# Block products for twelve slices of layer 0's second feed-forward, and where the weight sums are made

## The chip, the cores and the metric

The kernel runs on one core of a Trainium2 chip. The metric is the device time of one execution in microseconds, the median of several runs. TensorE does the matmuls and accumulates in PSUM banks of 512 float32 for each partition; VectorE (DVE) and ScalarE (ACT) do the elementwise work, each strictly in its own program order; GpSimd (POOL) here copies marks and starts some DMA transfers; SyncE (SP) starts the other transfers.

## What is computed

One inference step of a two-layer decoder over 1,024 prompt tokens and 8 sample rows. Layer 0 has a gated linear recurrence beside attention into 256 memory tokens, layer 1 stick-breaking attention beside memory attention; each is followed by the SwiGLU feed-forward that the change is about, in which `D_MODEL` is 1024 and `D_FF` is 2816:

```python
def swiglu(h, w_gu, w_down):
    gate, up = jnp.split(h @ w_gu, 2, axis=-1)
    return (jax.nn.silu(gate) * up) @ w_down
...
        h = h + rmsnorm(mix, g[1])
        h = h + rmsnorm(swiglu(rmsnorm(h, g[2]), w_gu[l], w_down[l]), g[3])
```

Everything is float32.

## The kernel before

**Tiling.** Activations lie transposed, features on the 128 partitions and tokens along the free axis. The tokens are two groups: group 0 holds 512 prompt tokens, group 1 the other 512 and the 8 sample rows, 520 columns that are worked on as two halves of 260 (`PW[1]`). A float32 product is made of reduced-precision ones (`float32r`): weight and activation are each split into a high and a low part, and three matmuls stand for one (high by high, high by low, low by high).

**A plain slice.** The feed-forward takes its 2,816 hidden features in 22 slices of 128. For one slice `split_w` (L250) loads weights as raw tiles of 128 x 512 from the pool `wraw` (5 tiles, on SP's queue), makes the high part on ScalarE (L260) and the low part on VectorE (L261) into the pool `wspl` (5 tiles); `proj` (L266) multiplies (L274). Gate and up have two such tiles each, so a slice of group 1 has four weight tiles, each used for 4 x 3 x 2 = 24 matmuls of 260 columns: 96 in all. The result lies in a `mm` tile, two PSUM banks wide, of which the pool `mmp` has two. `silu` (L284) works by exponential and logarithm.

**Parts.** The 22 slices are cut into parts of 5, 5, 4, 4 and 4 (`PARTS`). After a part's slices come its eight down projections, which add into the residual rows `R` (`class ffn`, L688; the addition is L447 in `evac_raw`). The part is the unit in which feed-forwards are interleaved with attention: each stage is a generator, and `weave` takes turns between generators by the number of steps given with each, so the program order of every engine is fixed when the program is written. The order of the whole is at L1488 to L1525. `f1 = ffn(1, 0, o1.x)` (L1500), layer 0's feed-forward for group 1, is the one whose last three parts the change touches; its first two run beside `b0.sb()` and `b0.mem()`, layer 1's attention for group 0 (matmuls L862 and L903, maximum L867, exponential L873, scaling L877 and L879, transposition L889).

**Block products.** Layer 1's feed-forward for group 1 (`class ffn_w`, L617) makes all slices but the first four in another way. The gate and up projections of a slice are one product of a 2 x 2 block matrix of weights (gate and up by first and second 512 features of `D_MODEL`) with a 2 x 2 block matrix of activations (first and second 512 features by first and second 260 columns). `gate_up_w` (L524) makes it of 7 block products in place of 8. Four of the seven weights are sums of blocks, three are blocks themselves; four of the seven operands are sums of activation blocks, three the blocks themselves. A block product has one weight tile of 128 x 512, used for 4 x 3 = 12 matmuls of 260 columns, so a slice has 84. Its seven products go into four accumulators, `pa` to `pd`, and between the products ScalarE writes negated copies into an accumulator before it is accumulated further (L559 and L562), and silu of `pa` (L565), a copy of `pd` (L568), an addition (L570), a subtraction (L572) and a second silu (L574) follow:

```python
        product(pa, 0, True)
        nc.scalar.activation(pb[:, :h], pa[:, :h], AF.Copy, scale=-1.0)
        product(pd, 1, True)
        product(pb, 2)
        nc.scalar.activation(pc[:, :h], pb[:, :h], AF.Copy, scale=-1.0)
        product(pa, 3)
        ...
        product(pb, 4)
        ...
        nc.vector.tensor_add(gt[:, h:n], dt[:, h:n], pb[:, :h])
        product(pc, 5)
        nc.vector.tensor_sub(gt[:, :h], pc[:, :h], dt[:, h:n])
        product(pb, 6)
```

The silu there is ScalarE's own table function, whose table is loaded by an instruction of its own (`ACT_TABLE_LOAD`) when the function changes. In that stage the other PSUM pools are closed, and each accumulator has two banks of its own (`quads`, L1523). Raw tiles come from `wraw` and, every second one, from halves of the pool `apool`; split tiles come from `wspl` and, three of eight, from `cpool`. Operand sums are made by `sums_w` (L326): for each of four blocks of 128 features 4 additions, 4 subtractions and 4 splits.

**Weight sums.** `weight_sums` (L588) makes the sums of weight blocks in DRAM (`wsum`), a part at a time, by eight transfers on GpSimd's queue: copies (L608) and transfers that add to what is there (L606). Each waits for a mark: ScalarE copies a column (L602) of what was made last, the number `self.now` that `ffn` keeps, into a small tile `rr`, GpSimd copies that (L603), and the transfer is issued after it. Before, the 40 transfers for layer 1's 22 slices are interleaved with parts 0 to 4 of `f1`.

**PSUM around the change.** Eight banks: `mmp` two tiles of two banks, `smp` three small banks (`S()`: attention's scores and transpositions), `nsp` one.

Of the kernel before, what the change touches and what calls it, by code (L numbers as in the profile page):

```python
# [24 lines left out]
def tile_decoder(  # L25
# [61 lines left out]
    def Q(i):  # L87
        return single[0].tile([P, 512], F32, tag=f"q{i}", name=nm("q"))
# [139 lines left out]
    def chain(*gens):  # L228
        for g_ in gens:
            yield from g_  # L230
# [16 lines left out]
    def sv(ap, g):  # L247
        return ap[:, :G] if g == 0 else ap.rearrange("p (a n) -> p a n", a=2)

    def split_w(W, k0, nk, m0):  # L250
        out = []
        for a in range(0, nk, 4):
            n = min(4, nk - a)
            raw = wraw.tile([P, 4, P], F32, tag="w", name=nm("w"))
            nc.sync.dma_start(
                raw[:, :n, :],
                W[(k0 + a) * P : (k0 + a + n) * P, m0 : m0 + P].rearrange("(k p) m -> p k m", p=P),
            )
            ws = wspl.tile([P, 2, 4, P], F32R, tag="ws", name=nm("ws"))
            nc.scalar.copy(ws[:, 0, :n, :], raw[:, :n, :])  # L260
            nc.vector.tensor_sub(ws[:, 1, :n, :], raw[:, :n, :], ws[:, 0, :n, :].bitcast(F32))  # L261
            for i in range(n):
                out.append((ws[:, 0, i, :], ws[:, 1, i, :]))
        return out
# [58 lines left out]
            out.append(x)  # L323
            yield

    def sums_w(xs, ops):  # L326

        n, h = NG[1], PW[1]  # L330
        for k in range(4):
            x0, x1 = xs[k], xs[k + 4]
            y = YT()
            if k % 2 == 0:
                z, u = YT(), YT()
            o = (k % 2) * h

            def full(x, c):
                t = B()
                nc.vector.tensor_add(t[:, :h], x[:, 0, c : c + h].bitcast(F32), x[:, 1, c : c + h].bitcast(F32))  # L340
# [13 lines left out]
            yield  # L354

    def YT():
        return xpool.tile([P, 2, NG[1]], F32R, tag="x0", name=nm("y"))

    def wo_tiles(g):
# [161 lines left out]
        split_to((mt[:, 0, :n], mt[:, 1, :n]), sg[:, :n])  # L521
        return mt, last

    def gate_up_w(l, f, ops, spl, raws):  # L524

        h, n = PW[1], NG[1]
        part, o = part_of(f)
# [26 lines left out]
                        start=(first and k == 0 and wi == 0), stop=(k == 3 and wi == 2), skip_group_check=True,  # L554
                    )

        pa, pb, pc, pd = (Q(i) for i in range(4))
        product(pa, 0, True)
        nc.scalar.activation(pb[:, :h], pa[:, :h], AF.Copy, scale=-1.0)  # L559
        product(pd, 1, True)  # L560
# [10 lines left out]
        product(pc, 5)  # L571
        nc.vector.tensor_sub(gt[:, :h], pc[:, :h], dt[:, h:n])  # L572
        product(pb, 6)
        nc.scalar.activation(sg[:, h:n], gt[:, :h], AF.Silu)  # L574
# [4 lines left out]
        return mt  # L579

    sums = {}

# [2 lines left out]
            if f0 <= f < f0 + nf:  # L585
                return i, (f - f0) * P

    def weight_sums(l, parts, after):  # L588

        for i in parts:  # L590
            f0, nf = PARTS[i]
            w = nf * P
            s1, s2, s3, s4 = (tc.dram_tile([512, w], F32, name=nm("wsum")) for _ in range(4))
            sums.setdefault(l, {})[i] = (s1, s2, s3, s4)
            a11, a12 = (w_gu[l][r : r + 512, f0 * P : f0 * P + w] for r in (0, 512))
            a21, a22 = (w_gu[l][r : r + 512, DFF + f0 * P : DFF + f0 * P + w] for r in (0, 512))
            for d, a, add in (
                (s3, a11, False), (s1, a21, False), (s3, a21, True), (s1, a22, True),
                (s2, s3, False), (s2, a22, True), (s4, s2, False), (s4, a12, True),
            ):  # L600
                tok = small([P, 1], tag="rr")
                nc.scalar.copy(tok, after())  # L602
# [12 lines left out]
    class ffn_w:  # L615


        def __init__(self, l, x, plain):
            self.g, self.l, self.x, self.ops, self.plain, self.n, self.r, self.pi = 1, l, x, [], plain, 0, 0, 0
            self.R = self.acc = None  # L620
            self.half = []
            self.sums = sums_w(x, self.ops)

        def spl(self):
            self.n += 1
# [13 lines left out]
        def part(self, pi):  # L639
# [4 lines left out]
            for j in range(nf):  # L644
# [5 lines left out]
                        for _ in range((1, 2, 1, 0)[j]):  # L650
                            next(self.sums, None)
                else:
                    mids.append(gate_up_w(l, f0 + j, self.ops, self.spl, self.raws))
                yield
            if pi == 0:
                self.R = R_one()
# [29 lines left out]
            yield from finish_rows(self)  # L686

    class ffn:  # L688
        def __init__(self, g, l, xt, rows=False):
            self.g, self.l, self.xt, self.rows = g, l, xt, rows  # L690
            self.R = self.acc = None

        def part(self, pi):
            g, l = self.g, self.l
# [2 lines left out]
            last = pi == len(PARTS) - 1  # L697
            mids = []
            for j in range(nf):
                pg = proj(g, w_gu[l], 0, ND, (f0 + j) * P, self.xt)  # L700
                sg = silu(None, pg, g)
                pu = proj(g, w_gu[l], 0, ND, DFF + (f0 + j) * P, self.xt)
# [4 lines left out]
                self.now = sg[:, 0:1]  # L707
                yield
            if pi == 0:
                self.R = R_one()  # L710
            if last:
                self.acc = small([P, WID], tag="st", bufs=3)
            for m in range(ND):
                ps = proj(g, w_down[l], f0, nf, m * P, mids)
                evac_raw(g, self.R, ps, m, self.acc, pi == 0, last)
                self.now = self.R[m][:, 0:1]
                if last and self.rows:
                    nc.scalar.activation(
                        self.R[m][:, :n], self.R[m][:, :n], AF.Copy, scale=gcol(l, 3, m)
# [1 line left out]
                    if m == 3:  # L721
                        first_half(self)
                if m % 2:
                    yield

        def finish(self, store):
# [749 lines left out]
    )  # L1476
    a0.open()
    a1 = mixer_a(1, x1)
    weave((chain(a0.gate(), a0.merge()), 8), (start(1, x1), 14))
    weave((a0.mem(), 8), (a1.fq(), 8))  # L1480
    o0 = out_proj(0, 0, M)
    drain(o0.mm(a0.xo))
    weave((o0.finish(), 17), (chain(a1.v(), a1.qm(A)), 8))
    f0 = ffn(0, 0, o0.x)
    weave((a1.core(), 22), (f0.part(0), 9))
    a1.open()
    weave((a1.sample(), 6), (a1.gate(), 4), (f0.part(1), 9))
    weave((chain(a1.merge(), a1.mem()), 12), (a1.mem_sample(), 20), (chain(f0.part(2), f0.part(3)), 16))  # L1488
    drain(f0.part(4))
    xk0, xb0 = [], []  # L1490
    o1 = out_proj(1, 0, M)
    drain(o1.mm(a1.xo, 0, 1))
# [66 lines left out]
```

## Times and profile before

| | |
|---|---|
| median of 3 runs | 2498.32 us (2496.75 to 2498.65) |
| the profiled execution | 2499.1 us, with a span of 2497.4 us |
| TensorE: busy, granted clock | 2462.8 us, 0.997 of full speed |
| VectorE, ScalarE, GpSimd busy | 1571.8, 1183.0, 98.3 us |
| moved by DMA | 358.21 MB |

Times come from one execution that the hardware profiler recorded; L274 is line 274 of the kernel before. A row of a group gives line, engine, operation, the tile written and the tiles read, their shapes, the number of instructions, then their busy time, the mean of one in ns, and the engine's idle time ahead of them with what ended it. Matmuls overlap, and their ends are modelled, so their mean is longer than the time that each adds. A row of the order of time gives start, duration, engine, line, operation and how many instructions are put together in it. A row by windows gives the window, its length, and the busy time of PE, weight loads, DVE, ACT and POOL with the number of instructions, the granted clock, the share of the DMA engines and GB/s.

### The profile page before, as it was taken

The page shows a single profiled execution, that of the slowest core. Times are in us where ns is not written, and L with a number is a line of the kernel's source. Part 1 is how long each engine was busy: PE and PEld are TensorE (multiplying, and loading weights), DVE is VectorE, ACT ScalarE, POOL GpSimd, SP SyncE. Part 2 cuts the span into 40 slices and gives each one's busy share as a digit, 9 for nine tenths or more (in the row PEclk, how much of TensorE's full clock was granted, in tenths as well). Part 3 has the DMA queues.
Part 4 walks back from the last instruction along what each step waited for, and adds up shares of the span by engine and source line. Part 5 has one row for each costly group of instructions (what it writes and reads, how often), then busy time and mean ns, then how long its engine had stood idle before and what let it go on. Part 6 is the DMA issues. An engine that isn't in the chain of part 4 may idle for free.

```text
span 2497.4 us, 40764 instructions
## 1 busy us (share of the span) xinstructions
PE 2462.8 (99%) x15565; PEld 2169.9 (87%) x15565; DVE 1571.8 (63%) x2756; ACT 1183.0 (47%) x2277; POOL 98.3 (4%) x139
## 2 busy tenths in 40 slices
PE   8999999999999999999999999999999999999998
PEld 6888988877877897999999989877787797999997
DVE  5766556655765585655544575777577648755655
ACT  5446543243433454555433454555444445564444
POOL 1000000000000000010111100022000000000000
PEclk9999999999999999999999999999999999999999
DMA  5352252233643447586678976544454234365542
GB/s 186 114 165 68 72 156 81 60 110 116 184 124 98 129 138 227 156 195 177 173 191 215 234 193 196 160 142 138 121 149 130 85 115 122 121 192 145 151 137 69
DMA packets 496110, 358.21 MB, mean 143 GB/s; under 512 B 19110, under 2 KB 443635, under 8 KB 495915
## 3 DMA queue, kind: packets, MB, share of 16 engines
q1 hardware_dynamic: 477354, 301.08, 40.5%
q0 software_dynamic: 18560, 54.53, 9.1%
q8 instruction: 122, 2.00, 0.3%
q14 instruction: 74, 0.60, 0.1%
HBM read 325.73 MB, written 75.94 MB: 161 GB/s over the span
## 4 chain that ended last, share of the span: by engine, by line
PE 88%; DVE 5%; DMA 3%; ACT 2%; issue 2%; POOL 0%; SPq 0%; DVEq 0%; ACTq 0%; POOLq 0%
PE mm L274 59%; PE q L552 7%; PE q L667 5%; PE s L1180 2%; PE q L510 2%; PE mm L1048 2%; PE s L903 1%; PE s L862 1%; PE mm L812 1%; DMA b<-qd 1%; PE mm L839 1%; DVE ws L261 1%; PE ns L957 1%; PE s L1336 1%; DMA c<-in_cache_sb_v,pidx 1%
## 5 line engine op out<-in xcount | busy, mean ns | idle before, releaser
L274 PE MATMUL mm<-x,ws 128*128 128x260 f32 (+1 forms) x7776 | 1332.9, 330 | 0.0
L274 PEld LDWEIGHTS mm<-x,ws 128*128 128x128 f32 x7776 | 1148.3, 188 | 151.5 <-issue 12.0
L260 ACT CAST ws<-w 128x512 fp32r<-128x512 f32 x712 | 420.2, 591 | 763.2 <-PE mm L274 620.2
L261 DVE TENSOR_TENSOR ws<-w,ws 128x512 fp32r<-128x512 f32 x712 | 462.5, 653 | 286.8 <-ACT ws L260 278.3
L274 PE MATMUL mm<-m,ws 128*128 128x512 f32 (+1 forms) x2112 | 393.5, 343 | 0.1
L274 PEld LDWEIGHTS mm<-m,ws 128*128 128x128 f32 x2112 | 324.4, 189 | 49.9 <-issue 2.6
L667 PE MATMUL q<-m,ws 128*128 128x260 f32 x1056 | 128.8, 283 | 0.0
L667 PEld LDWEIGHTS q<-m,ws 128*128 128x128 f32 x1056 | 127.2, 188 | 0.4 <-ACT hT L485 0.2
L543 DVE TENSOR_TENSOR ws<-w,ws 128x512 fp32r<-128x512 f32 x126 | 86.6, 691 | 61.5 <-ACT ws L542 59.3
L552 PE MATMUL q<-y,ws 128*128 128x260 f32 x864 | 112.9, 283 | 0.0
L542 ACT CAST ws<-w 128x512 fp32r<-128x512 f32 x126 | 78.0, 621 | 69.6 <-PE q L667 27.4
L552 PEld LDWEIGHTS q<-y,ws 128*128 128x128 f32 x864 | 107.6, 189 | 0.0
L291 DVE TENSOR_SCALAR t<-mm 128x512 f32<-128x512 f32 (+1 forms) x82 | 56.7, 692 | 79.6 <-PE mm L274 79.6
L447 DVE TENSOR_TENSOR r<-r,mm 128x512 f32<-128x512 f32 (+1 forms) x96 | 66.0, 688 | 61.1 <-PE mm L274 60.3
L703 DVE TENSOR_TENSOR t<-t,mm 128x512 f32<-128x512 f32 (+1 forms) x66 | 45.5, 690 | 74.2 <-PE mm L274 73.9
L295 DVE TENSOR_TENSOR t<-t,t 128x512 f32<-128x512 f32 (+1 forms) x66 | 45.8, 694 | 70.6 <-ACT t L294 70.6
L552 PE MATMUL q<-x,ws 128*128 128x260 f32 x648 | 86.3, 282 | 0.0
L552 PEld LDWEIGHTS q<-x,ws 128*128 128x128 f32 x648 | 81.3, 188 | 0.0
L314 DVE TENSOR_TENSOR st<-st,n 128x512 f32<-128x512 f32 (+1 forms) x98 | 67.1, 691 | 8.8 <-ACT n L313 7.0
L281 ACT CAST m<-t 128x512 fp32r<-128x512 f32 (+1 forms) x88 | 54.9, 624 | 18.1 <-DVE t L703 8.9
L282 DVE TENSOR_TENSOR m<-t,m 128x512 fp32r<-128x512 f32 (+1 forms) x88 | 61.0, 693 | 2.6 <-ACT m L281 1.4
L984 POOL DMA_INDIRECT c<-in_cache_sb_k,pidx x16 | 16.4, 1026 | 1170.5 <-ACT n L313 958.6
(339 smaller groups left out, 2557.9 us busy)
## 6 DMA issues: line engine op xcount, KB each, us to landing
w<-in_w_gu SPq DMA_DIRECT2D x334, 256.0 KB, 3.4
w<-in_w_down SPq DMA_DIRECT2D x160, 256.0 KB, 3.5
w<-in_w_in_a SPq DMA_DIRECT2D x80, 256.0 KB, 3.0
wsum<-in_w_gu POOLq DMA_DIRECT2D x18, 1024.0 KB, 9.5
w<-wsum SPq DMA_DIRECT2D x72, 256.0 KB, 3.8
w<-in_w_o SPq DMA_DIRECT2D x64, 256.0 KB, 2.8
wsum<-in_w_gu POOLq DMA_DIRECT2D x12, 1280.0 KB, 10.7
w<-in_w_mem_kv SPq DMA_DIRECT2D x32, 256.0 KB, 3.2
```

What stands on the lines that cost most here:

```text
L260: nc.scalar.copy(ws[:, 0, :n, :], raw[:, :n, :])
L261: nc.vector.tensor_sub(ws[:, 1, :n, :], raw[:, :n, :], ws[:, 0, :n, :].bitcast(F32))
L274: nc.tensor.matmul(ps[:, a, : PW[g]], wt, xt[k][:, xi, o : o + PW[g]], start=(k == 0 and wi == 0), stop=(k == nk - 1 and wi == 2),)
L281: nc.scalar.copy(dst[0], src)
L282: nc.vector.tensor_sub(dst[1], src, dst[0].bitcast(F32))
L291: nc.vector.tensor_scalar(sv(x, g), pv(ps, g), -44.0, None, op0=ALU.max)
L314: nc.vector.tensor_add(acc[:, :n], acc[:, :n], t[:, :n])
L447: nc.vector.tensor_add(dst, dst, pv(ps, g))
L542: nc.scalar.copy(w[:, 0, :], src)
L543: nc.vector.tensor_sub(w[:, 1, :], src, w[:, 0, :].bitcast(F32))
L552: nc.tensor.matmul(ps[:, :h], w[:, wj, k * P : (k + 1) * P], x[:, xi, :], start=(first and k == 0 and wi == 0), stop=(k == 3 and wi == 2), ...
L667: nc.tensor.matmul(pp[a][:, :h], wt, mids[k][:, xi, a * h : (a + 1) * h], start=(k == 0 and wi == 0), stop=(k == nf - 1 and wi == 2),)
```

## The change

Three things change together.

1. `f1`, layer 0's feed-forward for group 1, gets `prod=10`: its parts 2 to 4 (slices 10 to 21, twelve slices) are made by `gate_up_w`. Raw tiles come from `wraw` alone; split tiles from `wspl` and `cpool` (three of eight). Two accumulators (`pa`, `pd`) are small banks of `smp`, the two others (`pb`, `pc`) the halves of one `mm` tile. The operand sums are made in the down projections of part 1, one block after every second projection, into tiles of `apool`. ScalarE's table for exponential and logarithm is loaded again behind the last slice's gate.
2. Layer 0's weight sums for parts 2 to 4, 24 transfers, are added; they are interleaved with the memory attention, output projection and recurrence of the first half and with `f0.part(0)`. Layer 1's 40 move forward: 24 beside `f0.part(2)` to `f0.part(4)` of group 0 and 16 beside parts 0 and 1 of `f1`. In parts 2 to 4 of `f1` none are left.
3. The mark ahead of each of these transfers now reads the first column of the weight tile that was split last (`now[0]`, set in `split_w`).

```diff
+            now[0] = ws[:, 0, 0, 0:1].bitcast(F32)
...
-    def sums_w(xs, ops):
+    def sums_w(xs, ops, YT):
...
-        pa, pb, pc, pd = (Q(i) for i in range(4))
+        pa, pb, pc, pd = quads()
...
-                nc.scalar.copy(tok, after())
+                nc.scalar.copy(tok, now[0])
...
-        def __init__(self, g, l, xt, rows=False):
-            self.g, self.l, self.xt, self.rows = g, l, xt, rows
+        def __init__(self, g, l, xt, rows=False, prod=NF):
+            self.g, self.l, self.xt, self.rows, self.prod = g, l, xt, rows, prod
             self.R = self.acc = None
+            self.ops, self.n = [], 0
+            self.sums = sums_w(xt, self.ops, lambda: A(F32R))
+
+        def spl(self):
+            self.n += 1
+            if self.n % 8 in (1, 4, 6):
+                return cpool.tile([P, 2, 512], F32R, tag="c", name=nm("ws"))
+            return wspl.tile([P, 2, 512], F32R, tag="ws", name=nm("ws"))
+
+        def quads(self):
+            t = mmp.tile([P, 2, 512], F32, tag="mm", name=nm("mm"))
+            return S(), t[:, 0, :], t[:, 1, :], S()
...
+                if f0 + j >= self.prod:
+                    mt, gate = gate_up_w(
+                        l, f0 + j, self.ops, self.spl,
+                        lambda: wraw.tile([P, 4, P], F32, tag="w", name=nm("w")), self.quads,
+                    )
+                    mids.append(mt)
+                    yield
+                    continue
...
+            if last and self.prod < NF:
+                with tc.issue_after(gate.ins):
+                    nc.scalar.preload_act_table_set("natural_log_exp_and_others")
...
                 if m % 2:
+                    if f0 + nf == self.prod < NF:
+                        next(self.sums, None)
                     yield
...
+    ws = weight_sums(0, (2, 3, 4))
     weave((chain(a0.gate(), a0.merge()), 8), (start(1, x1), 14))
-    weave((a0.mem(), 8), (a1.fq(), 8))
+    weave((a0.mem(), 8), (a1.fq(), 8), (islice(ws, 6), 6))
     o0 = out_proj(0, 0, M)
-    drain(o0.mm(a0.xo))
-    weave((o0.finish(), 17), (chain(a1.v(), a1.qm(A)), 8))
+    weave((o0.mm(a0.xo), 8), (islice(ws, 6), 6))
+    weave((o0.finish(), 17), (chain(a1.v(), a1.qm(A)), 8), (islice(ws, 6), 6))
     f0 = ffn(0, 0, o0.x)
-    weave((a1.core(), 22), (f0.part(0), 9))
+    weave((a1.core(), 22), (f0.part(0), 9), (ws, 6))
...
-    weave((chain(a1.merge(), a1.mem()), 12), (a1.mem_sample(), 20), (chain(f0.part(2), f0.part(3)), 16))
-    drain(f0.part(4))
+    ws = weight_sums(1, range(5))
+    weave(
+        (chain(a1.merge(), a1.mem()), 12), (a1.mem_sample(), 20), (chain(f0.part(2), f0.part(3)), 16), (islice(ws, 16), 17)
+    )
+    weave((f0.part(4), 8), (islice(ws, 8), 8))
...
-    f1 = ffn(1, 0, o1.x)
-    ws = weight_sums(1, range(5), lambda: f1.now)
-    weave((chain(b0.sb(), b0.mem()), 24), (chain(f1.part(0), f1.part(1)), 18), (islice(ws, 16), 17))
-    weave((chain(f1.part(2), f1.part(3), f1.part(4)), 24), (ws, 24))
+    f1 = ffn(1, 0, o1.x, prod=10)
+    weave((chain(b0.sb(), b0.mem()), 24), (chain(f1.part(0), f1.part(1)), 18), (ws, 17))
+    drain(f1.part(2), f1.part(3), f1.part(4))
```

More of the change, by code (lines that the diff above doesn't have):

```diff
@@ L248, in sv @@
         return ap[:, :G] if g == 0 else ap.rearrange("p (a n) -> p a n", a=2)
+    now = [None]
     def split_w(W, k0, nk, m0):
@@ L354, in sums_w, with Y0 @@
             yield
-    def YT():
+    def Y0():
         return xpool.tile([P, 2, NG[1]], F32R, tag="x0", name=nm("y"))
@@ L522, in gate_up_q, with gate_up_w @@
         return mt, last
-    def gate_up_w(l, f, ops, spl, raws):
+    def gate_up_w(l, f, ops, spl, raws, quads):
         h, n = PW[1], NG[1]
@@ L573, in gate_up_w @@
         product(pb, 6)
-        nc.scalar.activation(sg[:, h:n], gt[:, :h], AF.Silu)
+        last = nc.scalar.activation(sg[:, h:n], gt[:, :h], AF.Silu)
         nc.vector.tensor_mul(sg[:, :h], sg[:, :h], pb[:, :h])
@@ L578, in gate_up_w @@
         split_to((mt[:, 0, :n], mt[:, 1, :n]), sg[:, :n])
-        return mt
+        return mt, last
     sums = {}
@@ L586, in part_of, with weight_sums @@
                 return i, (f - f0) * P
-    def weight_sums(l, parts, after):
+    def weight_sums(l, parts):
         for i in parts:
@@ L621, in __init__ @@
             self.half = []
-            self.sums = sums_w(x, self.ops)
+            self.sums = sums_w(x, self.ops, Y0)
         def spl(self):
@@ L652, in part @@
                 else:
-                    mids.append(gate_up_w(l, f0 + j, self.ops, self.spl, self.raws))
+                    mids.append(gate_up_w(
+                        l, f0 + j, self.ops, self.spl, self.raws, lambda: [Q(i) for i in range(4)]
+                    )[0])
                 yield
@@ L706, in part @@
                 mids.append(mt)
-                self.now = sg[:, 0:1]
                 yield
+            if last and self.prod < NF:
+                with tc.issue_after(gate.ins):
+                    nc.scalar.preload_act_table_set("natural_log_exp_and_others")
             if pi == 0:
@@ L715, in part @@
                 evac_raw(g, self.R, ps, m, self.acc, pi == 0, last)
-                self.now = self.R[m][:, 0:1]
                 if last and self.rows:
```

## The prediction

> **What bounds the kernel now.** I read the page first: the span, the busy shares, and the chain of waits.
>
> ```profile
> span 2497.4 us, 40764 instructions
> PE 2462.8 (99%) x15565; PEld 2169.9 (87%) x15565; DVE 1571.8 (63%) x2756; ACT 1183.0 (47%) x2277; POOL 98.3 (4%) x139
> ...
> PE 88%; DVE 5%; DMA 3%; ACT 2%; issue 2%; POOL 0%; SPq 0%; DVEq 0%; ACTq 0%; POOLq 0%
> ```
>
> TensorE is busy nearly always, and 88% of the chain that ended last is its work. So a change pays through fewer matmuls, and costs through every moment in which TensorE waits. What one matmul costs is not its mean time, since matmuls overlap. The group by form, TensorE's order of time in the stage that is changed, and two windows show it (in the windows x is the number of instructions; the first lies in that stage, the second in layer 1's block products).
>
> ```profile
> L274 PE MATMUL mm<-x,ws 128*128 128x260 f32 x4608 | 575.2, 285 | 0.0
> ...
> 1307.47 46.07 PE L274 MATMUL mm<-x,ws 128*128 128x260 f32 x384
> 1353.38 23.20 PE L274 MATMUL mm<-m,ws 128*128 128x260 f32 x192
> ...
> 1300.00:1400.00 100.00, 100.00 (x838) 100.00 (x838) 46.93 (x69) 37.82 (x69) 14.42 (x23) 1.00 0.87 218
> 2300.00:2400.00 100.00, 100.00 (x835) 100.00 (x834) 61.44 (x114) 50.78 (x101) 0.00 (x0) 1.00 0.51 149
> ```
>
> The mean is 285 ns, but 384 matmuls (four slices of 96) take 1353.38 - 1307.47 = 45.91 us: 0.1196 us each, 11.48 us a slice. Layer 1's block products run at the same price (100 / 835 = 0.1198 us) with TensorE full. The clock is 1.00 in both.
>
> **What the change removes.** Twelve slices go from 96 matmuls to 7 x 4 x 3 = 84: 144 x 0.1196 = 17.2 us less. Down projections keep their matmuls, and TensorE's order before this stage stays as it was. This is the whole gain; all that follows can only eat it.
>
> **What a slice now needs.** It splits seven weight tiles in place of four, and each feeds 12 matmuls (1.43 us) instead of 24. The prices are those of layer 1's block products, from the groups of instructions of 2163.8 to 2420 us; below them the time from issue to landing in that stretch (first two rows), between 1245 and 1510 us where the weight sums run (third), and over the whole run for another weight (fourth).
>
> ```profile
> L543 DVE TENSOR_TENSOR ws<-w,ws 128x512 fp32r<-128x512 f32 x103 | 70.8, 691 | 51.4 <-ACT ws L542 49.5 <-DMA w<-in_w_down 1.1
> L542 ACT CAST ws<-w 128x512 fp32r<-128x512 f32 x104 | 64.3, 621 | 58.8 <-PE q L667 27.4 <-PE q L552 15.6 <-DMA w<-wsum 8.5
> L570 DVE TENSOR_TENSOR t<-t,q 128x260 f32<-128x260 f32 x14 | 5.9, 419 | 0.3 <-PE q L552 0.3
> L572 DVE TENSOR_TENSOR t<-q,t 128x260 f32<-128x260 f32 x14 | 6.0, 428 | 1.2 <-PE q L552 1.0
> L574 ACT ACTIVATE t<-t 128x260 f32<-128x260 f32 x14 | 5.9, 418 | 3.0 <-DVE t L572 3.0
> L559 ACT ACTIVATE q<-q 128x260 f32<-128x260 f32 x15 | 5.6, 372 | 5.4 <-PE q L552 5.4
> L565 ACT ACTIVATE t<-q 128x260 f32<-128x260 f32 x14 | 5.4, 388 | 9.2 <-PE q L552 9.2
> L568 ACT COPY t<-q 128x260 f32<-128x260 f32 x14 | 5.2, 371 | 0.0
> ...
> w<-wsum SPq DMA_DIRECT2D x65, 256.0 KB, 3.9
> w<-in_w_gu SPq DMA_DIRECT2D x49, 256.0 KB, 3.9
> ...
> w<-in_w_gu SPq DMA_DIRECT2D x37, 256.0 KB, 6.7
> ...
> w<-in_w_in_a SPq DMA_DIRECT2D x80, 256.0 KB, 3.0
> ```
>
> By sums of work there is room: seven splits take ACT 7 x 0.62 = 4.3 us and DVE 7 x 0.69 = 4.8 us of a slice of 84 x 0.1196 = 10.05 us. By chains there isn't, for two reasons.
>
> First, layer 1 has `wraw` and half of `apool` for raw weights, and four accumulator banks with a buffer each. Here five `wraw` tiles are all, and the third and fourth accumulators `pb`, `pc` are halves of one `mm` tile. In the changed program TensorE's sixth product (into `pc`) waits for the vector add L570 that reads `pb`, and the seventh (into `pb`) for the subtraction L572 that reads `pc`. The order puts 8 and 5 matmuls of the next slice in between (0.96 and 0.60 us); the second gap needs about 0.2 (drain: a matmul's mean of 0.285 less its 0.12) + 0.43 + a hand-over, so some 0.2 us is lost a slice.
>
> Second, a raw tile is free only after its DVE split, lands 3.9 us later, and ScalarE and VectorE take splits and evacuations strictly in the order written, in which weights for the slice after next stand ahead of this slice's evacuations. The chain, from the end of one slice's sixth product to the end of the next one's: drain 0.2, cast 0.62, silu L574 0.42, negation L559 0.37, cast 0.62, DVE split 0.69 (which frees a tile) = 2.9; load 3.9; cast of it 0.62; only behind it silu L565 0.39, copy L568 0.37, cast 0.62, split 0.69, add L570 0.42 = 3.1; then the sixth product 1.43. That is 11.4 us against 10.05: 1.3 us lost. The same working for the other slices, by their orders, gives 1.0 and 1.3 in the first part of four slices, 1.9 and 0.5 in the second, 1.1 and 1.3 in the third; each part's last slice is followed by 24-matmul tiles and loses nothing. Sum 7.1, with 6 x 0.2 for the rest **8.3 us**. Bounds: 0 if the landing is short, and with 6.7 us five of these chains lose 2.8 more each, 22 us.
>
> The Trainium skill, "DMA: Bandwidth & Descriptors" (section "Anatomy of one DMA"), fits a transfer on the GpSimd path as 2.0 us plus bytes / 436 GB/s, 2.6 us for 256 KB by estimate. The rows say 3.9 us with this kind of traffic, on SP's queue, and the measurement decides; by the page nearly all of these losses would vanish.
>
> **The hand-over to the first product.** Before, attention's last softmax ran behind matmuls of the first plain slice (order of time, both engines' rows together).
>
> ```profile
> 1235.70 1.13 PE L903 MATMUL s<-b,c 128*128 128x256 f32 x4
> 1236.11 0.68 DVE L867 TENSOR_REDUCE nmx<-s 128x2 f32<-128x512 f32 x1
> 1236.48 2.14 PE L274 MATMUL mm<-x,ws 128*128 128x260 f32 x15
> 1236.83 0.48 ACT L873 ACTIVATE b<-s,nmx 128x256 f32<-128x256 f32 x1 [1.18 <-DVE nmx L867]
> ...
> 1237.88 0.17 DVE L877 RECIPROCAL sme<-sme 128x2 f32<-128x2 f32 x1 [1.09 <-ACT b L873]
> 1238.08 0.82 DVE L879 TENSOR_SCALAR b<-b,sme 128x256 f32<-128x256 f32 x2
> 1238.69 0.33 PE L889 MATMUL s<-ident,b 128*128 128x128 f32 x1
> ...
> 1239.26 0.96 PE L274 MATMUL mm<-x,ws 128*128 128x260 f32 x6
> ```
>
> The first product now needs a small bank, which attention's exponentials (L873) release. So the 15 matmuls move behind the transposition L889, and TensorE waits from 1236.5 to 1238.7 and longer, because two weight splits and a split of sums now stand ahead on both engines: I put it at 1239.5. That is 3.0 us, where 0.4 was idle (15 matmuls from 1236.48 end at 1238.28): **2.6 us**. Bounds: 0, if another filler is found, to 4.5 with every inserted split serial.
>
> **The operand sums** (64 instructions in the last eight projections of the second part).
>
> ```profile
> 1198.00:1241.00 43.00, 42.93 (x319) 40.60 (x317) 23.64 (x50) 18.15 (x47) 4.43 (x6) 1.00 0.78 188
> ...
> L340 DVE TENSOR_TENSOR b<-x 128x260 f32<-128x260 f32 x16 | 6.2, 422 | 0.0
> ...
> L602 ACT COPY rr<-r 128x1 f32<-128x1 f32 x12 | 2.2, 186 | 1.0 <-DVE r L447 0.3
> ...
> DVE c L955 <- DMA c<-in_cache_mem_v: 6.9, 5, 2.7
> ...
> L517 ACT ACT_TABLE_LOAD x1 | 1.3, 1283 | 0.0
> ```
>
> Forty-eight vector instructions at about 0.34 us back to back (6.2 us busy for 16 overlapping ones is 0.39) are 16 to 19 us; VectorE has 43 - 23.6 = 19.4 us free there. They fit, with no room left: 0 to 3 us of waits, I take **0.5**.
>
> **The weight sums** become 64 transfers instead of 40, with 24 more ScalarE marks of 0.19 us (4.5 us over 600 us, covered by an engine 47% busy), and run from the first memory attention on. Their weights feed 24 matmuls a tile there, so a landing of 6.7 us fits five tiles; in the window above such traffic left TensorE full. Exposed are the sample rows' cache loads, for which VectorE waits already (6.9 us in 5 waits), with splits queued behind. From 0 to 5 us; **0.5**. Leaving the later stage gives back nothing, as TensorE was full there. Two activation-table loads (1.3 us each) fall in ScalarE's gaps.
>
> **Sum:** -17.2 + 8.3 + 2.6 + 0.5 + 0.5 = -5.3 us on the profiled execution's 2499.1 us: 2493.8. The median is 0.8 lower, so about **2493.5 us**.
>
> **Rivals.** *The full gain:* short landings (3.0 us as for the input weights) save 0.9 on five chains, and with a filled hand-over little is lost: 2481 to 2487, middle 2484. For: layer 1's products never waited. Against: they had more raw tiles. The 2.6 us of the Trainium skill's page "DMA: Bandwidth & Descriptors" belong here. *Slower by the raw ring:* place, five `wraw` tiles in parts 2 to 4; price, five times the landing beyond 3.9 us. At 6.7 us it costs 14 more: 2508. It decides from 3.9 + 5 / 5 = 4.9 us, where nothing is gained. For: 6.7 us was measured for these very weights, and loads per microsecond rise by half. Against: then the sums' transfers were under way, now they are done. *Sums in the first half hurt:* 5 us at the cache loads, no more gain: 2499.
>
> **How the numbers follow.** Forecast (2488 to 2499) 0.46, full gain 0.20, slow ring (2500 to 2512, landings of 5.2 to 7.6 us) 0.26, first half 0.08. A measurement here tells 0.2% from nothing, 2493.3 to 2503.3. Faster: 0.20 and half of the forecast, 0.43. Slower: most of the slow ring and a third of the first half, 0.24. Same: the rest, 0.33. Range 2482 to 2510, which cuts the ends of both rivals; the forecast's own is 2488 to 2499.
>
> **What would show it.** Parts 2 to 4 lay between these rows of TensorE's order of time.
>
> ```profile
> 1240.96 43.64 PE L274 MATMUL mm<-x,ws 128*128 128x260 f32 x362
> ...
> 1445.37 5.01 PE L274 MATMUL mm<-x,ws 128*128 128x512 f32 x21
> ```
>
> In the same parts after: 1,008 block-product matmuls in place of 1,152; idle TensorE of 8 us there, mostly ahead of products 5 and 6 and put down to L559/L562 negations and the L570 add; ScalarE casts waiting for w landings of 3.9 us. About 2.6 us idle ahead of L889. If TensorE is full in these parts, the chain was wrong; if landings are 6 us, the ring wins; if idle time appears before 900 us, the sums do.

## The result, and the profile after

The changed kernel takes 2521.45 us (median of 6 runs, 2517.14 to 2527.91), the kernel before 2497.64 us beside it (2496.26 to 2499.86): 1.0096 of the time, interval 1.0083 to 1.0110. It is slower, and 11 us beyond the end of the range. The profiled execution is the longest of the six (2527.91 us), so its losses add up to some 6 us more than the median's. Line numbers of the profiles from here on are those of the changed kernel, up to some 30 higher; a kernel of an experiment may shift them by a few more.

The page of the changed kernel: its span, the busy shares, the granted TensorE clock in 40 slices, and the chain by engine.

```profile
span 2526.2 us, 40875 instructions
PE 2462.1 (97%) x15421; PEld 2158.4 (85%) x15421; DVE 1600.9 (63%) x2852; ACT 1211.7 (48%) x2379; POOL 124.2 (5%) x187
PEclk9999999999989999999999999999999999999998
...
PE 85%; DVE 6%; DMA 6%; ACT 2%; issue 1%; SPq 0%; POOL 0%; DVEq 0%; ACTq 0%
```

TensorE has its 144 matmuls less (15565 to 15421), and is yet busy for the same time. Transfers have gone from 3% to 6% of the chain, and one slice of the clock, near 730 us, has lost a tenth.

**Where the time went.** TensorE's order is the same in both kernels up to the first block product, so its n-th matmul of the one can be set beside the n-th of the other. The changed kernel is 5.6 us late at 568 us of its own time (2.2 us since 342 us, where TensorE waits for loads of residual rows, and 3.0 in two windows of halved clock at 533 and 561 us), 41.4 us late at 829 us, 39.3 us at the head of the stage with the block products, and 31.9 us at its end; a further 3 us come back in small amounts before the end of the kernel. So the stage gains 7.4 us (209.9 us before, 202.5 after), and nearly all the loss lies between 600 and 830 us. The windows of that stretch (PE, weight loads, DVE, ACT, POOL, clock, DMA share, GB/s), one row of before and then three of after:

```profile
700.00:800.00 100.00, 99.28 (x426) 73.41 (x425) 67.56 (x112) 38.91 (x84) 0.00 (x0) 1.00 0.41 121
```

```profile
600.00:700.00 100.00, 95.82 (x466) 77.42 (x465) 60.82 (x96) 37.49 (x74) 6.64 (x11) 1.00 0.70 201
700.00:800.00 100.00, 83.43 (x335) 62.17 (x334) 50.53 (x82) 33.51 (x76) 9.48 (x16) 0.91 0.77 205
800.00:900.00 100.00, 93.06 (x393) 70.78 (x392) 52.17 (x87) 38.53 (x81) 10.71 (x18) 0.98 0.75 198
```

The DMA share goes from 0.41 to 0.77, TensorE does 335 matmuls in place of 426, and the clock falls to 0.91. What TensorE and VectorE wait for, from the views of waits between 600 and 860 us (engine, what waits, for what: us in total, times, longest):

```profile
PE ns L985 <- DVE c L984: 12.9, 2, 9.1
PE mm L277 <- DVE t L294: 5.5, 2, 4.1
PE mm L277 <- ACT m L284: 3.4, 2, 2.2
```

```profile
DVE c L983 <- DMA c<-in_cache_mem_v: 39.8, 7, 9.2
DVE c L971 <- DMA b<-qd: 9.8, 3, 7.0
```

VectorE waits 39.8 us for the value cache of the sample rows, where it waited 6.9 us before, and 9.8 us for their queries (`b<-qd`), where it waited 1.7. TensorE's own waits end at the product that reads the scaled cache (L985) and at silu's work on earlier products (L294, L284, L728), which stands behind those loads in the order of VectorE and ScalarE; none that the view lists ends at a weight split. The value loads are not the whole loss, either: 9.2 of the 35.8 us are lost by 711 us of the changed kernel's time, before the first value load is issued at 727 us. The chain that ended last in 660 to 830 us (start, duration, what) runs there through a load of the queries and a weight of group 0's down projections, and only then through value loads, the first of which is shown:

```profile
663.00 14.06 DMA b<-qd
...
693.37 11.16 DMA w<-in_w_down
...
729.00 16.17 DMA c<-in_cache_mem_v
```

One of the value loads, in order of time on SP's queue, VectorE and TensorE:

```profile
747.72 1.86 PE L985 MATMUL ns<-c,sel 128*8 128x512 f32 x2 [9.05 <-DVE c L984]
...
758.80 0.37 SPq L1000 DMA_DIRECT2D c<-in_cache_mem_v  x1
...
769.08 1.23 DVE L983 TENSOR_TENSOR c<-c,ss 128x1024 f32<-128x1024 f32 x1 [9.16 <-DMA c<-in_cache_mem_v]
770.22 0.68 DVE L263 TENSOR_TENSOR ws<-w,ws 128x512 fp32r<-128x512 f32 x1
```

Issued at 758.80, in use at 769.08: 10.3 us, where the median from issue to landing of this load was 3.8 us before. Right behind it in VectorE's order stands a weight split (L263), which needs nothing of the cache and waits all the same. The share of the 16 DMA engines in 40 slices of 680 to 800 us, of before and then of after:

```profile
DMA  6343333356067505537052442347033584232203
```

```profile
DMA  9999999999997989999984035399942369970349
```

The engines are full for half of the stretch. The Trainium skill, "DMA: Bandwidth & Descriptors" (sections "Queues, rings and completion order" and "Issuing engines are not separate DMA queues"), says that transfers of all issuing engines share the same 16 DMA engines, and that each of these takes turns between queues, a whole packet at a time. The trace agrees with the sharing: the sums are issued by GpSimd, the cache loads by SP, and the second get slower when the first run. The turns packet by packet no run here shows.

**The clock.** Three windows in which it was halved:

```profile
707.50:710.90 3.40, 3.40 (x10) 2.62 (x9) 1.23 (x2) 0.70 (x2) 0.00 (x0) 0.51 1.10 212
741.70:751.90 10.20, 4.18 (x8) 2.03 (x9) 5.20 (x9) 1.02 (x4) 0.00 (x0) 0.50 0.32 93
792.90:796.30 3.40, 3.40 (x9) 2.63 (x8) 2.44 (x4) 2.64 (x6) 1.10 (x2) 0.50 0.29 84
```

They come during or after idle TensorE. With a fourth of 3.4 us at 823.6 us, TensorE was busy for 14.4 us of them (3.40 + 4.18 + 3.40 + 3.4) at half speed, so 7.2 us are lost to the clock, on top of the 27.5 us that all rows of its waits add up to: 34.7 of the 35.8 us by which this stretch got later. The Trainium skill, "TensorE: Matmul & The Clock Gate" (Part 1), gives a free-running window of about 3.4 us after which an idle array is clocked at half; lengths of 3.4 and three times 3.4 us agree. That only an idle array is slowed, this trace doesn't show: the two windows at 533 and 561 us, also 3.4 us each, lie where TensorE is busy throughout, and the clock of this stretch is 0.97 where it was 1.00 before.

```profile
500.00:600.00 100.00, 99.99 (x517) 76.51 (x517) 52.36 (x83) 39.67 (x66) 0.00 (x0) 0.97 0.37 110
```

**The stage that was changed.** A window in its middle, and TensorE's waits from 1235 to 1480 us:

```profile
1300.00:1400.00 100.00, 98.43 (x796) 96.06 (x795) 57.65 (x98) 45.61 (x91) 0.00 (x0) 1.00 0.48 139
```

```profile
PE s L917 <- DVE b L907: 2.2, 1, 2.2
PE mm L555 <- DVE t L575: 0.9, 1, 0.9
PE mm L555 <- DVE t L573: 0.6, 1, 0.6
```

The hand-over costs 2.2 us, as forecast (2.6). The only other waits that the view lists are those of the sixth and seventh products for the vector additions, 1.5 us. But 796 matmuls in 100 us are fewer than the 838 of before, and 1.5 us of waiting don't make up for 42 matmuls. The order of time of two slices' ends shows the rest (TensorE, and below it two instructions of VectorE):

```profile
1298.54 1.71 PE L555 MATMUL mm<-x,ws 128*128 128x260 f32 x12
1300.09 0.63 PE L555 MATMUL s<-x,ws 128*128 128x260 f32 x4
1300.56 0.28 PE L555 MATMUL s<-a,ws 128*128 128x260 f32 x1
1300.77 1.71 PE L555 MATMUL mm<-a,ws 128*128 128x260 f32 x12
1302.32 1.49 PE L555 MATMUL s<-a,ws 128*128 128x260 f32 x11
...
1300.29 0.43 DVE L575 TENSOR_TENSOR t<-mm,t 128x260 f32<-128x260 f32 x1 [1.21 <-PE mm L555]
```

The single matmul at 1300.56 stands 0.21 us ahead of the next, in place of 0.12: the seventh product begins at 1300.77, when the subtraction L575 has ended (1300.29 + 0.43). Twelve matmuls of it then take 1.55 us to the next start, not 1.44. Such steps are too short to be listed as waits. From all starts in the stage, idle time left out, a block-product matmul takes 124.9 ns where a plain one took 120.3, and one of the down projections 121.9 for 120.0: 1008 x 4.6 + 576 x 1.9 ns = 5.7 us.

### The profile page after: what moved, and what is told of

Read it like the earlier page. It is cut to its first block, busy times and chain, and to the rows that moved or that the text cites. A ratio compares the mean times of both kernels' runs of the same rounds, so it can differ in the third digit from the quotient of the medians.

```text
span 2526.2 us, 40875 instructions
## 1 busy us (share of the span) xinstructions
PE 2462.1 (97%) x15421; PEld 2158.4 (85%) x15421; DVE 1600.9 (63%) x2852; ACT 1211.7 (48%) x2379; POOL 124.2 (5%) x187
## 4 chain that ended last, share of the span: by engine, by line
PE 85%; DVE 6%; DMA 6%; ACT 2%; issue 1%; SPq 0%; POOL 0%; DVEq 0%; ACTq 0%
PE mm L277 52%; PE q L555 7%; PE q L672 5%; PE mm L555 2%; DMA c<-in_cache_mem_v 2%; PE s L1208 2%; PE q L513 2%; PE mm L1076 2%; PE s L555 2%; DMA b<-qd 1%; PE s L1364 1%; PE mm L840 1%; PE s L931 1%; PE mm L867 1%; PE s L1403 1%
## 5 line engine op out<-in xcount | busy, mean ns | idle before, releaser
L277 PE MATMUL mm<-x,ws 128*128 128x512 f32 (+1 forms) x6624 | 1197.8, 339 | 8.3 <-DVE t L294 5.5
L277 PEld LDWEIGHTS mm<-x,ws 128*128 128x128 f32 x6624 | 1011.8, 189 | 163.2 <-issue 18.3
L262 ACT CAST ws<-w 128x512 fp32r<-128x512 f32 (+1 forms) x664 | 390.1, 589 | 640.2 <-PE mm L277 511.3
L263 DVE TENSOR_TENSOR ws<-w,ws 128x512 fp32r<-128x512 f32 (+1 forms) x664 | 429.3, 650 | 274.2 <-ACT ws L262 265.7
L546 DVE TENSOR_TENSOR ws<-w,ws 128x512 fp32r<-128x512 f32 x210 | 144.1, 691 | 95.9 <-ACT ws L545 93.1
L545 ACT CAST ws<-w 128x512 fp32r<-128x512 f32 x210 | 129.4, 620 | 117.6 <-PE q L672 26.4
L450 DVE TENSOR_TENSOR r<-r,mm 128x512 f32<-128x512 f32 (+1 forms) x96 | 65.9, 687 | 42.9 <-PE mm L277 42.2
L294 DVE TENSOR_SCALAR t<-mm 128x512 f32<-128x512 f32 (+1 forms) x70 | 48.3, 691 | 61.8 <-PE mm L277 61.5
L606 POOL COPY mk<-rr 128x1 f32<-128x1 f32 x64 | 23.9, 374 | 1070.1 <-ACT rr L605 1070.1
L298 DVE TENSOR_TENSOR t<-t,t 128x512 f32<-128x512 f32 (+1 forms) x54 | 37.4, 692 | 54.0 <-ACT t L297 54.0
L728 DVE TENSOR_TENSOR t<-t,mm 128x512 f32<-128x512 f32 (+1 forms) x54 | 37.1, 688 | 51.7 <-PE mm L277 50.9
L284 ACT CAST m<-t 128x512 fp32r<-128x512 f32 (+1 forms) x88 | 54.8, 623 | 27.0 <-DVE t L728 17.0
L295 ACT ACTIVATE t<-t 128x512 f32<-128x512 f32 (+1 forms) x54 | 34.2, 634 | 63.2 <-DVE t L294 59.6
```

The lines of the kernel that those rows point to most:

```text
L277: nc.tensor.matmul(ps[:, a, : PW[g]], wt, xt[k][:, xi, o : o + PW[g]], start=(k == 0 and wi == 0), stop=(k == nk - 1 and wi == 2),)
L284: nc.scalar.copy(dst[0], src)
L450: nc.vector.tensor_add(dst, dst, pv(ps, g))
L545: nc.scalar.copy(w[:, 0, :], src)
L546: nc.vector.tensor_sub(w[:, 1, :], src, w[:, 0, :].bitcast(F32))
```

## The experiments

All are the changed kernel with one thing altered; "early" is its 24 transfers of layer 1's sums beside parts 2 to 4 of group 0's feed-forward, 16 of them beside the sample rows' memory attention.

**All sums moved, no block products.**

```diff
-    f1 = ffn(1, 0, o1.x, prod=10)
+    f1 = ffn(1, 0, o1.x)
```

> All 64 weight-sum transfers at their new places, but layer 0's second feed-forward stays plain (no block products, no operand sums). In the changed kernel's trace VectorE waits 39.8 us for the sample rows' value cache (6.9 before) between 660 and 830 us, while the sums' transfers fill the DMA engines. Theory A (the moved transfers delay the cache loads, VectorE's order passes it on to the weight splits, and the whole slowdown is there): 2525 to 2540 us, slower than the changed kernel, since only the gain of the products is missing. Rival B (the block products and their operand sums cost the time, the waits at the cache loads are covered elsewhere): 2497 to 2505 us.

2532.6 us, 1.0132 of before (1.0117 to 1.0148), and the same waits:

```profile
DVE c L983 <- DMA c<-in_cache_mem_v: 35.6, 7, 9.3
```

```profile
700.00:800.00 100.00, 86.42 (x341) 64.52 (x341) 50.42 (x82) 34.13 (x76) 9.68 (x16) 0.90 0.79 211
```

The plain stage takes its 209.9 us, as before. So the moved transfers alone cost 35.6 us, and the products gain.

**Layer 1's sums back beside the second feed-forward.**

```diff
-        (chain(a1.merge(), a1.mem()), 12), (a1.mem_sample(), 20), (chain(f0.part(2), f0.part(3)), 16), (islice(ws, 16), 17)
+        (chain(a1.merge(), a1.mem()), 12), (a1.mem_sample(), 20), (chain(f0.part(2), f0.part(3)), 16)
...
-    drain(f1.part(2), f1.part(3), f1.part(4))
+    weave((chain(f1.part(2), f1.part(3), f1.part(4)), 24), (ws, 24))
```

> The changed kernel with layer 1's 40 transfers back beside parts 0 to 4 of the second feed-forward, 24 of them beside the block products; layer 0's 24 stay at their new places. Theory A: the slowdown of 600 to 860 us goes, 2482 to 2492 us. Rival C (my prediction's raw ring: beside the sums' transfers a weight lands 6.7 us after its issue, and five chains of the ring lose 2.8 us more each): 2496 to 2508 us, with 10 to 20 us of idle TensorE in parts 2 to 4.

2542.21 us, 1.0184 (1.0170 to 1.0198): worse than the change. The first half is as before it (1.2 us early at 982 us), but the stage takes 254.1 us. A window there, what TensorE waits for, and what ScalarE's casts wait for:

```profile
1300.00:1400.00 100.00, 78.01 (x604) 75.64 (x603) 42.30 (x72) 34.47 (x78) 12.86 (x25) 0.93 0.79 204
```

```profile
PE mm L277 <- DVE r L450: 23.8, 5, 8.8
PE mm L555 <- ACT mm L562: 6.1, 1, 6.1
PE mm L555 <- ACT mm L565: 5.7, 3, 3.6
```

```profile
ACT ws L545 <- DMA w<-wsum: 50.9, 12, 12.3
ACT ws L545 <- DMA w<-in_w_gu: 21.0, 7, 10.8
```

Rival C had the place right and the price too low: weights are waited for up to 12.3 us. TensorE's longest waits, 23.8 us, are those of down projections for the addition L450, which stands behind such late weights' splits in VectorE's order. Theory A, which had only the cache loads in view, fell short. Plain slices stood in the same place beside 24 such transfers before, and lost nothing; that a raw tile feeds 24 matmuls there and 12 here is how I read it. Not separated here are ScalarE's waits for GpSimd's marks in the stage (L605 for L606, 9.6 us in all): the next run tests marks in the first half alone.

**The marks without transfers.** 24 marks stand early, ScalarE's and GpSimd's copies without a transfer, and layer 1's sums late.

```diff
+    def marks():
+        while True:
+            tok = small([P, 1], tag="rr")
+            nc.scalar.copy(tok, now[0])
+            nc.gpsimd.tensor_copy(small([P, 1], tag="mk", bufs=1), tok)
+            yield
```

> As the run with layer 1's sums late, but 24 marks (ScalarE's copy and GpSimd's copy, no transfer behind them) stand where the changed kernel has 24 of layer 1's sums. Theory A (the transfers cost the time): within 2 us of the run without these marks, 2482 to 2493 us. Rival D (the marks cost it, as more instructions in the order of ScalarE and GpSimd at the place where the sample rows wait): 2510 to 2525 us.

2542.73 us, against 2542.21 without them: the base was not where theory A had it, but the marks add nothing.

**Layer 0's sums left out**, layer 1's late.

```diff
-    ws = weight_sums(0, (2, 3, 4))
...
+        if l == 0:
+            f0, nf = PARTS[part]
+            b = w_gu[l][512:D, f0 * P : (f0 + nf) * P]
+            sums.setdefault(l, {})[part] = (b, b, b, b)
```

> As the run with layer 1's sums late, and layer 0's 24 transfers are left out: its block products load plain weight blocks in place of sums. Theory A (transfers beside other loads cost time wherever loads are waited for): 2 to 6 us less than with them, since TensorE's order is 4 us later by 540 us in the changed kernel. Rival E (at 215 to 490 us the transfers are hidden, and those 4 us come from elsewhere): within 1.5 us.

2545.87 us, 1.0190 (1.0176 to 1.0203), against 1.0184 with them: no gain, since the intervals overlap. The times so speak for rival E; theory A's 2 to 6 us are not there. By matched matmuls the 24 transfers aren't wholly hidden: between 340 and 400 us, where residual rows are loaded, each of the ten profiles with them gets later by 0.3 to 5.7 us (2.2 in the changed kernel), and this one, without them, by 0.1. The rest of the "4 us" of the expectation was mostly halved clock (1.5 us at 533 us of the changed kernel).

**Layer 1's sums in quieter places.**

```diff
+    ws = weight_sums(1, range(5))
+    weave((f0.part(4), 8), (islice(ws, 8), 8))
...
+    weave((b0.heads(), 8), (o1.finish(), 17), (islice(ws, 8), 8))
...
+    weave((chain(b0.sb(), b0.mem()), 24), (chain(f1.part(0), f1.part(1)), 18), (islice(ws, 16), 17))
...
+    weave((b1.heads(), 8), (o0.finish(), 17), (ws, 8))
```

> The changed kernel with layer 1's 40 transfers where neither the sample rows' cache loads nor block products wait for loads: none before the end of the sample rows' memory attention, 8 beside part 4 of group 0's feed-forward, 8 beside layer 1's queries, 16 beside parts 0 and 1 of the second feed-forward, 8 after it (beside the second group's queries). The run with layer 1's sums late showed TensorE 49 us later at the end of the block products, with weights waited for up to 12 us, and nothing lost before them. Theory A, widened (the transfers fill the DMA engines, and whatever load is waited for with little slack then comes late: cache loads in the first half, block-product weights in the second): 2483 to 2492 us. Rival F (the products themselves cost more than they save, wherever the sums are): 2497 us or more.

2519.85 us, 1.0074 (1.0061 to 1.0087): a miss. The early loss is gone, and another has come, in TensorE's order of time:

```profile
996.18 0.45 PE L430 MATMUL ns<-ident,ht 128*128 128x128 f32 x1 [10.13 <-DMA ht<-in_x_prompt]
```

The 8 transfers beside layer 1's queries meet the loads of the residual rows, which TensorE adds at once (L430); with what follows they cost 16 us between 874 and 1003 us of the kernel before. The 8 after the stage cost 7 us more, between 1563 and 1570 us. I had taken "quiet" from the DMA share, and not asked what is loaded there and how soon it is used.

**Other accumulators, same places.**

```diff
-            return S(), t[:, 0, :], t[:, 1, :], S()
+            return NS(), S(), t[:, 0, :], S()
```

> As the quiet placement, with other accumulators: pa in the bank of the norms' sums, which attention doesn't use, pb and pd in small banks, pc alone in a mm tile. The changed kernel's trace shows 2.2 us of idle TensorE at the hand-over and 1.5 us ahead of products that wait for L573 and L575. Theory A: those waits go, 2 to 4 us less than the quiet placement. Rival G (the small banks are then short for attention's tail, or the waits are covered): within 1 us or more.

2509.98 us, 10 less than the same placement, the stage 196.5 us for 203.8. This kernel doesn't compute the same values: pb lies in a small bank that attention's transpositions used before, and matmuls are to add there to a negated copy that ScalarE wrote. A likely cause, not shown: the Trainium skill, "PSUM — Partial Sum Buffer" (section "The four PSUM rules"), says that a matmul that doesn't begin a group adds where an earlier one has written and overwrites elsewhere, which no run here measures by itself. The run's time stands for the order of work alone.

**Half as many early.**

```diff
+        (chain(a1.merge(), a1.mem()), 12), (a1.mem_sample(), 20), (chain(f0.part(2), f0.part(3)), 16), (islice(ws, 8), 9)
...
+    weave((b0.heads(), 8), (o1.finish(), 17), (islice(ws, 8), 8))
```

> As the quiet placement, but 8 of layer 1's transfers (in place of the changed kernel's 16) stand beside the sample rows' memory attention, and none after the second feed-forward. Theory A (each transfer delays the cache loads it meets): 8 to 20 us more than the quiet placement, about half of the changed kernel's loss. Rival H (the loads are late only once the engines are full for long): within 4 us of the quiet placement.

2511.76 us, 1.0049 (1.0034 to 1.0063), 8 us less than the quiet placement: neither the 8 to 20 us more of theory A nor within the 4 us of rival H. The places of the sums differ from that run in more than the early 8: none stand behind the stage, where 8 cost 7 us. By matched matmuls the 8 early ones, spread over the same stretch at twice the distance, cost 7.8 us, where 16 cost 35.8: less than in proportion. Nearly all of the 7.8 is lost from 700 to 715 us of the kernel before, at a weight of the down projections (15.8 us from issue to use) and a load of the queries; at the value loads behind it, with three of the sums beside them, 0.5 us is lost, where the changed kernel lost 26.6. Another 9 us are again the residual rows' at 980 us.

**No sums for layer 1.**

```diff
+        if l == 1:
+            f0, nf = PARTS[part]
+            b = w_gu[l][512:D, f0 * P : (f0 + nf) * P]
+            sums.setdefault(l, {})[part] = (b, b, b, b)
```

> The changed kernel with layer 1's 40 transfers left out: layer 1's block products load plain weight blocks in place of sums. It shows what the block products in layer 0 are worth with only their own 24 sums. Theory A: 17.2 us of matmuls less 2.2 at the hand-over, 1.5 in the stage and 2 to 4 for the operand sums and layer 0's transfers: 2485 to 2491 us. Rival F (the products cost more than they save): 2497 us or more.

2490.98 us, 0.9973 (0.9962 to 0.9985). With layer 1's block products made of plain blocks, and so none of its 40 transfers, the block products, their own 24 sums and the shared tile gain 8.3 us against the 2499.24 of before in that run. By matched matmuls the stage itself gains 8.4; what comes and goes elsewhere nearly cancels. The stage's loads from issue to landing (the last column) between 1245 and 1440 us:

```profile
w<-wsum SPq DMA_DIRECT2D x40, 256.0 KB, 2.9
w<-in_w_gu SPq DMA_DIRECT2D x31, 256.0 KB, 3.0
```

**Places where nothing short of slack is loaded.**

```diff
+    w1 = weight_sums(1, range(5))
+    weave((a1.core(), 22), (f0.part(0), 9), (chain(ws, islice(w1, 8)), 14))
...
+    weave((f0.part(4), 8), (islice(w1, 8), 8))
...
+    weave((chain(b0.sb(), b0.mem()), 24), (chain(f1.part(0), f1.part(1)), 18), (islice(w1, 20), 21))
...
+    weave((o1.mm(b1.xo), 8), (w1, 5))
```

> The changed kernel with layer 1's 40 transfers in four stretches where the runs so far lost nothing: 8 beside part 0 of group 0's feed-forward, 8 beside its part 4, 20 beside parts 0 and 1 of the second feed-forward, 4 beside the last output projection. The quiet placement lost 17 us at 980 to 1005 us, where the residual rows are loaded while 8 transfers run, and 6 us at 1563 to 1590 us, where the other 8 ran; 9 of its own 16 others were lost nowhere. Theory A (a transfer costs time only beside a load that TensorE's work waits for soon: cache rows, residual rows, block-product weights): none of these losses, 2488 to 2497 us. Rival I (40 transfers cost what they cost, wherever they are): 2508 us or more.

2495.79 us, 0.9995 (0.9986 to 1.0004). The waits at the cache between 600 and 860 us, and a window in which 8 sums run beside a plain part:

```profile
DVE c L983 <- DMA c<-in_cache_mem_v: 6.8, 5, 2.9
```

```profile
800.00:900.00 100.00, 99.47 (x516) 83.55 (x515) 57.96 (x93) 46.70 (x89) 9.08 (x16) 1.00 0.83 223
```

The DMA share is 0.83 there (0.40 before), higher than in any window of the slow stretch, and TensorE stays full. Rival I falls, and so does the share of the engines as a measure: what waits for them decided here.

**The same places, each accumulator its own tile.**

```diff
-            t = mmp.tile([P, 2, 512], F32, tag="mm", name=nm("mm"))
-            return S(), t[:, 0, :], t[:, 1, :], S()
+            t, u = (mmp.tile([P, 2, 512], F32, tag="mm", name=nm("mm")) for _ in range(2))
+            return NS(), t[:, 0, :], u[:, 0, :], S()
```

> As the run before, with other accumulators: pa in the bank of the norms' sums, pb and pc in two mm tiles of their own, pd in a small bank. In the changed kernel a block-product matmul takes 125.0 ns from start to start where a plain one takes 120.3 ns; the excess lies in pairs of 0.2 us steps, one at the head of the sixth product and one at the seventh, beside 1.5 us of longer waits for L573 and L575 and 2.2 us at the hand-over. Theory J (pb and pc wait for each other's readers because they share a tile): 5 to 8 us less than the same placement with the shared tile, matmuls back at 120 to 122 ns. Rival K (the price is of the products themselves, or the two mm tiles make the next slice's negation wait for the gate of the slice before): within 2 us, or more.

2488.19 us, 0.9962 (0.9949 to 0.9976): 7.6 us less than with the shared tile, and faster than both kernels of this case. The same window in the stage, first with the shared tile (the run before this one) and then without, and the stage's waits without:

```profile
1300.00:1400.00 100.00, 99.57 (x808) 97.43 (x807) 57.70 (x97) 46.53 (x93) 0.00 (x0) 1.00 0.52 150
```

```profile
1300.00:1400.00 100.00, 100.00 (x833) 99.88 (x832) 59.77 (x101) 49.67 (x100) 0.00 (x0) 1.00 0.54 156
```

```profile
PE s L931 <- ACT b L922: 2.1, 1, 2.1
PE mm L555 <- ACT mm L562: 1.7, 2, 1.1
PE mm L555 <- DVE t L573: 0.7, 1, 0.7
PE mm L555 <- ACT mm L565: 0.4, 1, 0.4
```

833 matmuls in 100 us, for 808 with the shared tile in the same placement, 796 in the changed kernel and 838 plain. A block-product matmul takes 122.2 ns, so theory J's 5 to 8 us are met, and its 120 to 122 ns nearly. The steps of a tenth of a microsecond at the sixth and seventh products are nearly all gone, so I put them down to the shared tile; pa's bank changed in the same run, and was not tried alone. Less than half of the 7.6 us is that: 1008 x 2.7 + 576 x 1.6 ns makes 3.6 us against the changed kernel, and 2.1 us are given back, as negations now wait for a tile (L562, L565). The rest is the hand-over: TensorE's waits there are 5.0 us in the profile of the same placement with the shared tile, followed by 6.8 us at half clock, and 2.1 us without halved clock here. What is left of it wasn't pursued.

## Why the prediction was wrong

The step that failed is *the weight sums*: "From 0 to 5 us; 0.5". The place was named (the sample rows' cache loads, splits queued behind), and a late load that holds up VectorE's order is what happened; but the size was out by 30 us beyond the bound: all sums moved alone cost 35.6 us. The path was also wider than named: 9.2 of the changed kernel's 35.8 us there were lost at the sample rows' queries and at a weight of the down projections, and TensorE waited for the scaled cache itself and for silu's work on earlier products, not for splits. The bound of 5 was set by what VectorE already waited (6.9 us), as if the load beside them stayed as it was. The rows quoted had a better one. Beside the sums a weight landed in 6.7 us, and in 3.0 elsewhere; a cache load of 3.8 us would so take 3.8 x 6.7 / 3.0 = 8.5, 4.7 more, and eight value loads in a chain 37 us. The one shown took 10.3, and VectorE's waits for them grew by 33. That plain slices kept TensorE full beside such traffic was right of the window shown, and was no evidence for a load without slack. What I had no term for is the clock: 7 us of the 36.

- *144 matmuls, 17.2 us:* right, by count. The stage gave 7.4 us of it in the change.
- *The raw ring, 7.1 us:* not there. No wait of TensorE in the stage ends on a weight. The landing that I took, 3.9 us, was that of layer 1's stage; in this one it is 2.9 to 3.0 where the view gives it (the kernel without layer 1's sums), the end that I gave to the rival of the full gain. The estimate of 2.6 us from the fit of the Trainium skill ("DMA: Bandwidth & Descriptors", "Anatomy of one DMA") was nearer than my row from another stage. That the ring decides at longer landings was right: with sums beside it the stage lost 44 us (254.1 for 209.9, though it has 144 matmuls less).
- *The shared tile, 1.2 us:* the mechanism was right, the size wasn't. 1.5 us are listed as waits, and 5.7 lie in steps of a tenth of a microsecond, mostly at the heads of the sixth and seventh products, that no view of waits lists. I counted the second gap alone.
- *The hand-over, 2.6 us:* 2.2. *Operand sums, 0.5:* none to be seen; TensorE's delay is the same at 1005 and at 1235 us in the kernel without layer 1's sums. *Layer 0's sums:* nothing that the times can tell; 0.3 to 5.7 us at residual rows near 342 us by matched matmuls.
- *The sum of the stage* (-17.2 + 8.3 + 2.6 = -6.3) came out near its 7.4 by luck: two errors cancel, no ring and a dearer tile. The last line has a slip besides: 2493.8 less 0.8 is 2493.0, not 2493.5.
- *The rivals:* "sums in the first half hurt" is what happened, at seven times its price of 5 us, and I gave it 0.08. "Slower by the raw ring" didn't happen here, since the change had taken the sums out of that stage.

## What to carry to other kernels

A background transfer has no price of its own: it costs what it adds to the next load that something in order waits for. Before such work is moved, list the loads of the new place with their time from issue to use; a place with the engines 40% busy, 83% with the sums beside it, was free, and one at 41%, 77% with the sums, was not. Two accumulators in one tile waited here for each other's readers, so look at the matmuls per microsecond of a stage, and not only at its list of waits.

## What the runs showed of the hardware that was not expected

Waiting cost twice here: where TensorE waited 27 us in 600 to 830 us, the clock was halved for 20 us around the waits, which cost 7 us more. Not every halved window follows a wait, as the two at 533 and 561 us show; what brought those on stays open. And the price of traffic is not linear in the number of transfers: 8 beside the memory attention cost 7.8 us, 16 cost 35.8, in one profile each.
